# A hybrid two-layer decoder on one core: projection of token tile 0 between the norms, routing per token tile with a single gather, constant matmuls in PE's waits, and the last small-expert matmuls set behind the large ones

## Chip, cores and metric

One core of a Trainium2 chip runs the whole program. The metric is the device time of one execution in microseconds (us); where several executions are shown, their median counts. TensorE is called PE (its weight loads PEld), VectorE DVE, ScalarE ACT, GpSimd POOL, SyncE SP. SP's queue, in this kernel, does little else than start DMAs.

## What is computed

The input is x, 256 tokens of 1024 values in fp32. Each of two layers normalises x, projects it once into the inputs of four token mixers, merges their outputs through gates, projects and adds; then it normalises again and adds a feed-forward part, a dense one in layer 0 and a mixture of experts (MoE) in layer 1. Cut to that last part, where most of the time goes:

```
h = rmsnorm(x, gain)                       # 256 x 1024
logits = h @ router                        # 256 x 8
for each token: the 2 largest of 8 logits, weights = softmax of the two
y[token] = sum over its 2 experts e of weight * (silu(h @ w1[e]) * (h @ w3[e])) @ w2[e]
x = x + y                                  # w1, w3: 1024 x 3584, w2: 3584 x 1024, per expert
out = rmsnorm(x, gain)                     # after the last layer
```

All of it is fp32, and all weights come from HBM once per execution: 472 MB read.

## The kernel before

**Tiles.** The 256 tokens are two token tiles, t = 0 and 1, of 128. Weights arrive as `raw` tiles of 1 MB, one DMA each on SP's queue (`load_raw`, L125). There are 4 raw slots, 9 in the MoE part; SP starts the next load when a slot is free. A raw tile is split in two halves: ACT rounds a half to fp32r (`whi`, L164), DVE subtracts to get the remainder (`wlo`, L165). A precise product is then three matmuls, hi x hi, lo x hi, hi x lo (`mm3`, L156 to L158), or two in another arrangement (`both_parts`, L240 and L242). The activations are split in the same way: `hp`, `gTr` and `gTl`, `xer` and `xel`.

**Norms.** `norm_rows` (L193) squares on ACT, takes a square root on ACT and a reciprocal on DVE, and multiplies by x and the `gain` broadcast on DVE into `hh` (L207). `turn_half` (L217) turns hh by PE transposes into `pt`; ACT and DVE split that into `hp`. `norm_T` does both token tiles before it returns; the mixer layer begins with it. Its first product is `t_group(256, ...)`, whose matmuls write `pst`, 24 for each token tile; the next ones are `psw`. `small_loads` brings the layer's constants (sm, gln, bs, mc, cst) on POOL's queue.

**MoE.** `moe` (L667) normalises both token tiles (`hhm`), turns them (`hTm`), and multiplies by the router (`pl`, L696); the logits are turned back by a transpose (L699). DVE ranks the 8 logits (gt, eq, rank, `sel`); matmuls with a triangle and with ones give each token's position in its expert (`pp`) and the counts (`pc`). `order` sorts experts by count, so that large ones (128 slots) are paired with small ones (64 slots); `posp` are the positions in that order. `G` is the one-hot matrix of slots, and `psg` (L835) gathers the tokens: G times the split h (`htp`). Expert 0 always comes first, so its G needs no order: the kernel gathers expert 0's 128 slots first and the paired small expert's 64 in a second pass. `psgt` turns G. Loads of other experts' weights have addresses read from `ixi` on SP. `paired` then runs 28 steps, 4 pairs of 7 chunks: `psu` (large up), `psT`, `psd` (large down), `psq` (small up, plain fp32), `psTs`, `psds` (small down). `scatter_large` and `scatter_small` give the results back to tokens (`pssc`, two matmuls each, L899 and L900) and add to x (L902). `finish` normalises and stores.

**What sets the order.** Each engine runs its instructions in one list. A scheduler makes the lists when the program is built; by hand it is steered by `behind`, which keeps one instruction after another on the same engine, and by `hold_splits`, which holds back the splits of coming weights behind given instructions, but for the first few (`skip`).

Of the kernel before, what the change touches and what calls it, by code (L numbers as in the profile page):

```python
# [17 lines left out]
P = 128  # L18
# [77 lines left out]
def decoder_kernel(ctx, tc, x_in, consts_in, mconsts_in, bias_in, small_in, gln_in, gbs_in, norms_in, w_in,  # L96
# [24 lines left out]
    def load_raw(src, a, n):  # L121
# [3 lines left out]
        nc.sync.dma_start(raw, src)  # L125
        return raw

    def load_w(src, a, n):
# [3 lines left out]
        raw = load_raw(src, a, n)  # L132
# [17 lines left out]

    def w_rows(w, k0, nk, c0=0, n=D):
        return load_w(w[k0 * P:(k0 + nk) * P, c0:c0 + n].rearrange("(k p) n -> p k n", p=P), nk, n)

    def mm3(ps, lhs, rhs, start, stop):

        nc.tensor.matmul(ps, lhsT=lhs[0], rhs=rhs[0], start=start, stop=False)  # L156
        nc.tensor.matmul(ps, lhsT=lhs[0], rhs=rhs[1], start=False, stop=False)  # L157
        nc.tensor.matmul(ps, lhsT=lhs[1], rhs=rhs[0], start=False, stop=stop)  # L158
# [16 lines left out]
    nc.sync.dma_start(x[:, 0], x_in[0:P, :])  # L175
    gains = {0: gain_tile(0)}
    ident = cp.tile([P, P], F32, name="ident")
    make_identity(nc, ident)
# [4 lines left out]
    ones = cp.tile([P, P], F32, name="ones")  # L183
    nc.gpsimd.memset(ones, 1.0)
    cst = cp.tile([P, C_END], F32, name="cst")

    def sqrt_table(after, rows=slice(None)):

        junk = cp.tile([P, 1], F32, name="junk", tag="junk", bufs=2)
        nc.scalar.activation(junk[rows], after, AF.Sqrt, scale=0.0, bias=eps_l[rows])  # L190


    def norm_rows(ps, g, t, dst, done):  # L193
# [11 lines left out]
        for n in range(2):  # L205
            c = slice(n * 512, (n + 1) * 512)
            last = nc.vector.scalar_tensor_tensor(out=dst[:, c], in0=x[:, t, c], scalar=rs, in1=g[:, c],  # L207
                                                  op0=ALU.mult, op1=ALU.mult)
            done(n)
        return last  # L210

    def turn_half(hh, t, n):

        pt = psA.tile([P, 4, P], F32, name="pt", tag="mm")
        for k in range(4):
            kk = n * 4 + k
            nc.tensor.transpose(pt[:, k], hh[:, t, kk * P:(kk + 1) * P], ident)  # L217
        return pt

    def norm_T(ps, i):  # L220
# [6 lines left out]
        for t in range(TT):  # L227
# [4 lines left out]
            norm_rows(ps, g, t, hh[:, t], done)  # L232
        if ps is not None:
            hold_splits(ends, 2)
# [29 lines left out]
    def mixer_layer(l, h):  # L264
        with ExitStack() as lctx:
# [7 lines left out]
            def small_loads():  # L273
                q = nc.gpsimd
                q.dma_start(sm, small_in[l])
# [23 lines left out]
            def t_group(c0, evac):  # L299
                wt = [w_rows(win, 4 * i, 4, c0, 512) for i in range(2)]  # L300
                for t in range(TT):
# [4 lines left out]
                    evac(t, ps)  # L306
# [14 lines left out]
            t_group(256, evac_ab)  # L321
# [207 lines left out]
            units = [lambda: wq(0), lambda: wq(1), lambda: wk_(0), lambda: wk_(1), lambda: t_group(1792, evac_v)]  # L529
# [137 lines left out]
    def moe(i, norm_i, l, mT):  # L667
        with ExitStack() as lctx:
# [18 lines left out]
            for t in range(TT):  # L687
                def done(n):
                    marks["turned"] = nc.scalar.activation(hT[n][:, :, t * P:(t + 1) * P], turn_half(hh, t, n), AF.Copy)
                marks["normed"] = norm_rows(ps, g, t, hh[:, t], done)  # L690
            lgT = wk.tile([NE, T], F32, name="lgT", tag="gfs", bufs=1)
            for t in range(TT):
                tk = slice(t * P, (t + 1) * P)
                pl = psB.tile([NE, P], F32, name="pl", tag="ax")
                for k in range(KD):
                    nc.tensor.matmul(pl, lhsT=rt[:, k], rhs=hT[k // 4][:, k % 4, tk], start=k == 0, stop=k == KD - 1)  # L696
                nc.vector.tensor_copy(lgT[:, tk], pl)
                pl2 = psB.tile([P, NE], F32, name="pl2", tag="ax")
                nc.tensor.transpose(pl2, lgT[:, tk], ident[0:NE, 0:NE])  # L699
                nc.vector.tensor_copy(lg[:, t], pl2)  # L700
            halves = [slice(n * 512, (n + 1) * 512) for n in range(2)]
            with behind([marks["turned"], marks["normed"]]):
                for c in halves:
                    split(ht[0][:, 0, c], ht[1][:, 0, c], hh[:, 0, c])
            gains[norm_i + 1] = gain_tile(norm_i + 1)

            shp = [P, TT, NE, NE]
            oth = lg[:, :, None, :].to_broadcast(shp)
            own = lg[:, :, :, None].to_broadcast(shp)
            gt = wk.tile(shp, F32, name="gt", tag="rk", bufs=2)  # L710
            nc.vector.tensor_tensor(out=gt, in0=oth, in1=own, op=ALU.is_gt)
            eq = wk.tile(shp, F32, name="eq", tag="rk", bufs=2)
            nc.vector.tensor_tensor(out=eq, in0=oth, in1=own, op=ALU.is_equal)
            lt = cst[:, C_LT:C_LT + 64].rearrange("p (a b) -> p a b", a=NE)[:, None].to_broadcast(shp)
            nc.vector.tensor_tensor(out=eq, in0=eq, in1=lt, op=ALU.mult)
            nc.vector.tensor_tensor(out=gt, in0=gt, in1=eq, op=ALU.add)
            rank = small([P, TT, NE], "rank")
            nc.vector.tensor_reduce(out=rank, in_=gt, axis=AX.X, op=ALU.add)
            sel = small([P, TT, NE], "sel")
            nc.vector.tensor_scalar(out=sel, in0=rank, scalar1=1.5, scalar2=None, op0=ALU.is_lt)  # L720

            pp = psB.tile([P, TT, NE], F32, name="pp", tag="ax")
            tri = cst[:, C_TRI:C_TRI + 128]
            nc.tensor.matmul(pp[:, 0], lhsT=tri, rhs=sel[:, 0], start=True, stop=True)
            nc.tensor.matmul(pp[:, 1], lhsT=ones, rhs=sel[:, 0], start=True, stop=False)
            nc.tensor.matmul(pp[:, 1], lhsT=tri, rhs=sel[:, 1], start=False, stop=True)
            pc = psB.tile([P, NE], F32, name="pc", tag="ax")
            nc.tensor.matmul(pc, lhsT=ones, rhs=sel[:, 0], start=True, stop=False)
            nc.tensor.matmul(pc, lhsT=ones, rhs=sel[:, 1], start=False, stop=True)

            pos = small([P, TT, NE], "pos")
# [370 lines left out]
```

## Time and profile before

| what | us |
|---|---|
| median of 3 runs (1590.26 to 1591.65) | 1591.19 |
| profiled execution | 1589.84 |
| its span, first to last instruction | 1588.1 |
| layer 0's first psw starts | 31.43 |
| layer 1's first psw starts | 449.93 |
| first gather matmul psg starts | 669.31 |
| first psu starts | 683.72 |
| last matmul of the down projections starts its group | 1570.70 |

The page of the profile gives busy shares and groups; the waits list what an engine stood idle for (total, times, longest); the timeline gives single instructions with start, duration, engine, line, operation, what is written <- what is read, and in brackets the idle time before it with its releaser; a table by stretches (`A:B`) gives the busy time of each engine, the clock that was granted to PE (1.00 is full), the DMA share and GB/s. Matmul durations overlap, since they are pipelined: the distance between two starts tells the rate.

### The profile page before, as it was taken

Reading aid. Unit: us, or ns where it says so; the run is one execution under the profiler, and the core shown is the slowest. Engines: PE = TensorE matmul, PEld = TensorE weight load, DVE = VectorE, ACT = ScalarE, POOL = GpSimd, SP = SyncE. Lnnn points to the kernel's source line nnn. Section 1 sums busy time; section 2 is a strip of 40 time slices with the busy share of each in tenths; the row PEclk is TensorE's granted clock in tenths of the full one; section 3 lists DMA queues with packets and bytes.
Section 4 is the critical chain, followed back from the end, with each engine's and each line's share of the span. In section 5 each row is a group of like instructions: output and inputs, shape, how many; then the busy total and the mean of one; then the engine's idle time right before and its main releaser. Section 6 shows DMA issues by size and latency. Waiting matters only on the chain.

```text
span 1588.1 us, 20024 instructions
## 1 busy us (share of the span) xinstructions
PE 1531.3 (96%) x7508; PEld 1065.8 (67%) x7508; DVE 977.8 (62%) x1291; ACT 808.1 (51%) x1184; POOL 20.8 (1%) x47
## 2 busy tenths in 40 slices
PE   6999999999899999899999999999999999999997
PEld 5888897888788889776555555555555555555553
DVE  5896776665679777765445655454645554654444
ACT  5577746555464865554434534344434453444342
POOL 2000000000100000000000000000000000000000
PEclk9999999999999999989999999999999999999998
DMA  9565555555565645479998989999999999899993
GB/s 324 189 192 181 173 181 173 187 188 190 186 199 167 198 160 196 163 307 376 421 407 371 413 343 421 400 413 374 385 372 403 404 408 373 365 417 405 398 390 141
DMA packets 134890, 474.61 MB, mean 299 GB/s; under 512 B 7744, under 2 KB 77376, under 8 KB 91776
## 3 DMA queue, kind: packets, MB, share of 16 engines
q1 hardware_dynamic: 132512, 466.65, 76.2%
q0 software_dynamic: 1984, 6.08, 1.2%
q8 instruction: 61, 1.00, 0.3%
q10 hardware_dynamic: 288, 0.52, 0.1%
q14 instruction: 45, 0.37, 0.1%
HBM read 472.17 MB, written 1.05 MB: 298 GB/s over the span
## 4 chain that ended last, share of the span: by engine, by line
PE 89%; DVE 4%; ACT 4%; issue 2%; DMA 1%; SPq 0%; DVEq 0%; ACTq 0%
PE psw L240 16%; PE psq L923 14%; PE psw L242 8%; PE psu L157 7%; PE psu L158 7%; PE psu L156 6%; PE psds L944 5%; PE psd L157 3%; ACT whi L164 3%; PE psd L158 3%; DVE wlo L165 3%; PE psd L156 2%; PE psg L835 2%; PE psf L156 1%; PE psf L158 1%
## 5 line engine op out<-in xcount | busy, mean ns | idle before, releaser
L165 DVE TENSOR_TENSOR wlo<-raw,whi 128x1024 fp32r<-128x1024 f32 x546 | 647.7, 1221 | 252.8 <-ACT whi L164 249.6
L164 ACT ACTIVATE whi<-raw 128x1024 fp32r<-128x1024 f32 x546 | 554.0, 1053 | 130.4 <-PE psw L240 40.1
L240 PE MATMUL psw<-hp,whi 128*128 128x512 f32 x1088 | 388.6, 400 | 0.6 <-DVE hp L165 0.6
L242 PE MATMUL psw<-hp,wlo 128*128 128x256 f32 x1088 | 307.0, 282 | 0.0
L240 PEld LDWEIGHTS psw<-hp,whi 128*128 128x128 f32 x1088 | 205.1, 188 | 52.8 <-issue 3.3
L923 PE MATMUL psq<-raw,xs 128*64 128x512 f32 x896 | 218.6, 596 | 0.0
L242 PEld LDWEIGHTS psw<-hp,wlo 128*128 128x128 f32 x1088 | 206.3, 190 | 2.1 <-issue 1.1
L157 PE MATMUL psu<-wlo,xer 128*128 128x512 f32 x448 | 183.4, 409 | 9.5 <-DVE wlo L165 9.5
L156 PE MATMUL psu<-whi,xer 128*128 128x512 f32 x448 | 179.6, 401 | 1.3 <-DVE x L902 1.2
L158 PE MATMUL psu<-whi,xel 128*128 128x512 f32 x448 | 176.1, 393 | 0.0
L923 PEld LDWEIGHTS psq<-raw,xs 128*64 128x64 f32 x896 | 65.3, 137 | 129.0 <-issue 128.7
L925 ACT ACTIVATE gfs<-psq 64x512 f32<-64x512 f32 x28 | 16.5, 591 | 251.7 <-PE psq L923 251.7
L157 PEld LDWEIGHTS psu<-wlo,xer 128*128 128x128 f32 x448 | 84.6, 189 | 64.0 <-issue 30.0
L156 PEld LDWEIGHTS psu<-whi,xer 128*128 128x128 f32 x448 | 84.8, 189 | 41.9 <-ACT whi L164 17.0
L944 PE MATMUL psds<-raw,gTs 128*64 128x512 f32 x448 | 110.8, 604 | 0.0
L926 DVE TENSOR_TENSOR gfs<-gfs,psq 64x512 f32<-64x512 f32 x28 | 19.4, 692 | 137.7 <-ACT gfs L925 137.7
L158 PEld LDWEIGHTS psu<-whi,xel 128*128 128x128 f32 x448 | 84.8, 189 | 15.3
L157 PE MATMUL psd<-wlo,gTr 128*128 128x512 f32 x224 | 92.3, 412 | 2.1
L158 PE MATMUL psd<-whi,gTl 128*128 128x512 f32 x224 | 88.1, 393 | 0.0
L259 ACT ACTIVATE sum<-psw 128x256 f32<-128x256 f32 x120 | 44.8, 374 | 67.0 <-PE psw L242 67.0
L156 PE MATMUL psd<-whi,gTr 128*128 128x512 f32 x224 | 75.4, 413 | 2.7 <-ACT whi L164 2.7
L872 ACT ACTIVATE gfm<-psu 128x512 f32<-128x512 f32 x28 | 16.7, 597 | 119.9 <-PE psu L158 119.9
(260 smaller groups left out, 1570.4 us busy)
## 6 DMA issues: line engine op xcount, KB each, us to landing
raw<-in_moe_w_dram SPq DMA_DIRECT2D x336, 1024.0 KB, 8.2
raw<-in_dense_w_dram SPq DMA_DIRECT2D x33, 1024.0 KB, 5.3
raw<-in_w_gate_dram SPq DMA_DIRECT2D x32, 1024.0 KB, 5.4
raw<-in_w_in_dram SPq DMA_DIRECT2D x22, 1024.0 KB, 5.6
raw<-in_w_out_dram SPq DMA_DIRECT2D x8, 1024.0 KB, 5.0
raw<-in_w_br_c_dram SPq DMA_DIRECT2D x4, 1024.0 KB, 5.5
s<-in_bias_dram POOLq DMA_DIRECT2D x16, 192.0 KB, 4.2
gain<-in_norms_dram SPq DMA_DIRECT2D x5, 512.0 KB, 4.9
```

Of the source, the lines that this page charges most:

```text
L156: nc.tensor.matmul(ps, lhsT=lhs[0], rhs=rhs[0], start=start, stop=False)
L157: nc.tensor.matmul(ps, lhsT=lhs[0], rhs=rhs[1], start=False, stop=False)
L158: nc.tensor.matmul(ps, lhsT=lhs[1], rhs=rhs[0], start=False, stop=stop)
L164: return (nc.scalar.activation(hi, src, AF.Copy), nc.vector.tensor_tensor(out=lo, in0=src, in1=hi.bitcast(F32), op=ALU.subtract))
L165: nc.vector.tensor_tensor(out=lo, in0=src, in1=hi.bitcast(F32), op=ALU.subtract))
L240: nc.tensor.matmul(ps.rearrange("p a t -> p (a t)"), lhsT=w[0], rhs=act[:, k].rearrange("p a t -> p (a t)"), start=start, stop=False)
L242: nc.tensor.matmul(ps[:, 1], lhsT=w[1], rhs=act[:, k, 0], start=False, stop=stop)
L259: nc.scalar.activation(out[:, b], ps[b][:, 1], AF.Copy)
L835: nc.tensor.matmul(ps[:, b, cs], lhsT=ht[part][:, t, k * P:(k + 1) * P], rhs=self.G[:, t].rearrange("p s n -> p (s n)")[:, cs], start=n == ...
L923: nc.tensor.matmul(ps[rows], lhsT=xs[:, kk], rhs=w[:, k], start=kk == 0, stop=kk == KD - 1)
L926: nc.vector.tensor_tensor(out=gf[HI], in0=gf[HI], in1=ps[HI], op=ALU.mult)
L944: nc.tensor.matmul(acc["s"][rows], lhsT=gT[:, 2 * j + k], rhs=w[:, k, n * 512:(n + 1) * 512], start=c == 0 and j == 0 and k == 0, stop=c = ...
```

## The change

Six edits:

- **Start.** The gain of layer 0's first norm is no longer loaded as a 128 x 1024 broadcast. One row of 4 KB is loaded, and two matmuls with ones (`spread`) put it into PSUM, where DVE reads it. x's tile 0 comes in two halves, the first two raws in two pieces each, in the order row, x0, raw0, x1, raw1. The square-root table of ACT is loaded by an extra instruction ahead of the norm. Six one-element copies on POOL from raw1 into sm, gln, bs, mc and cst make the loads of these wait for raw1's first piece; the bias loads `s` stand ahead of them now.
- **Projection between norms.** `norm_T` takes a function that it calls after token tile 0; both mixer layers issue the 24 `pst` matmuls of tile 0 there, before tile 1's norm.
- **Routing per token tile.** gt, eq, rank, sel, off, pos, pp and pc are made for each token tile, at half the width, as soon as its logits are there.
- **One gather.** `order` and posp come first; G is made once for the large and the small expert, and psg runs once, 192 columns wide. Index loads from ixi are made at first use, not all at once. The splits of weights wait behind the gather's, where two raws had been split ahead.
- **Constant matmuls.** `keep_busy` multiplies ones by ones (`idle`, 128x128): 9 at the start, and 5, 3, 3, 8 and 12 in the routing.
- **The end.** The last small down projection (`psds`) is kept behind the last large one (`psd`).

```
+    def keep_busy(after, n):
+        ps = psB.tile([P, P], F32, name="idle", tag="ax")
+        for j in range(n):
+            with behind([after] if after else []):
+                after = nc.tensor.matmul(ps, lhsT=ones, rhs=ones, start=j == 0, stop=j == n - 1)
+        return after
+    busy = keep_busy(None, 6)
...
+            busy = nc.tensor.matmul(spread[n], lhsT=ones[0:1], rhs=row[:, n * 512:(n + 1) * 512], start=True, stop=True)
+    keep_busy(busy, 3)
...
             norm_rows(ps, g, t, hh[:, t], done)
+            if t == 0 and between:
+                between(h)
         if ps is not None:
-            hold_splits(ends, 2)
+            hold_splits(ends, 0 if between else 2)
...
+                if l == 0:
+                    for dst in (sm, gln, bs[:, 0], bs[:, 1], mc, cst):
+                        q.tensor_copy(dst[:, 0:1], early_raw[:, 1, 0:1])
...
-            t_group(256, evac_ab)
+            part = t_group(256, evac_ab)
+            evacs = []
+            h = norm_T(ps, 2 * l, lambda h: evacs.append(part(h, 0)))
+            evacs[0]()
+            part(h, 1)()
...
+            place, pm = order()
+            posp = by_place(pos, pm, "posp")
             first = Slots()
-            first.one_hot(0, pos[:, :, 0:1])
-            place, pm, ixi = order()
-            posp = by_place(pos, pm, "posp")
-            first.inputs(0, NSLOT)
-            first.one_hot(1, posp[:, :, NE // 2:NE // 2 + 1])
-            hold_splits([marks["G"]], 2)
...
-            first.inputs(NSLOT, NSLOT + NSMALL)
-            first.turned()
+            first.one_hot(None, posp[:, :, 0:NE:NE // 2])
...
+            expert(NE // 2)
+            first.inputs(0, NSLOT + NSMALL)
+            hold_splits(marks["x"], 2)
...
-                down_small(place_of[NE - 1], nch - 1, gTs)
+                with behind(ends):
+                    down_small(expert(NE - 1), nch - 1, gTs)
```

The lists of the engines show the moves. Each row has the line (those of the changed kernel are other numbers), the operation, what is written <- what is read, and the shape of the output.

SP's list at the very start, before; `in_w_in` is the mixers' input projection:

```order
L175 DMA x<-in_x_dram 128x1024
L172 DMA gain<-in_norms_dram 128x1024
L1040 DMA x<-in_x_dram 128x1024
L125 DMA raw<-in_w_in_dram 128x4x512 x2
L125 DMA raw<-in_w_in_dram 128x8x256 x2
```

and after:

```order
L190 DMA row<-in_norms_dram 1x1024
L192 DMA x<-in_x_dram 128x512 x2
L129 DMA raw<-in_w_in_dram 128x2x512 x2
L1114 DMA x<-in_x_dram 128x1024
L129 DMA raw<-in_w_in_dram 128x2x512 x2
L129 DMA raw<-in_w_in_dram 128x8x256 x2
```

The gain broadcast has gone, and the first raw stands ahead of x's second tile.

PE's list in the routing, from the transposes of the normed tokens to the first large up projection, before:

```order
L217 MATMUL pt<-ident,hhm 128x128 x8
L696 MATMUL pl<-hTm,rt 8x128 x8
L217 MATMUL pt<-ident,hhm 128x128 x8
L699 MATMUL pl_6270<-ident,lgT 128x8
L696 MATMUL pl<-hTm,rt 8x128 x8
L699 MATMUL pl_6283<-ident,lgT 128x8
L724 MATMUL pp<-sel,cst 128x8
L728 MATMUL pc<-sel,ones 128x8
L835 MATMUL psg<-G,htp 128x128 x32
L851 MATMUL psgt<-ident,G 128x128 x4
L835 MATMUL psg<-G,htp 128x64 x32
L156 MATMUL psu<-whi,xer 128x512
```

and after:

```order
L248 MATMUL pt<-ident,hhm 128x128 x8
L209 MATMUL idle<-ones 128x128 x5
L755 MATMUL pl<-hTm,rt 8x128 x8
L248 MATMUL pt<-ident,hhm 128x128 x8
L760 MATMUL pl_6310<-ident,lgT 128x8
L776 MATMUL pc<-sel,ones 128x8
L778 MATMUL pp<-sel,cst 128x8
L755 MATMUL pl<-hTm,rt 8x128 x8
L209 MATMUL idle<-ones 128x128 x12
L898 MATMUL psg<-G,htp 128x192 x32
L914 MATMUL psgt<-ident,G 128x128 x4
L163 MATMUL psu<-whi,xer 128x512
```

Left out are rows of the same kind (idle groups of 3, 3 and 8 and the rest of pp and pc). The router's matmuls of tile 1 now stand behind pc and pp of tile 0, and one gather stands where two stood.

PE's list at the end of the last step, before; the two psd are the two halves of the large expert's output:

```order
L944 MATMUL psds<-raw,gTs 64x512 x4
L157 MATMUL psd_11115<-wlo,gTr 128x512
L158 MATMUL psd_11115<-whi,gTl 128x512
L157 MATMUL psd_11116<-wlo,gTr 128x512
L158 MATMUL psd_11116<-whi,gTl 128x512
L944 MATMUL psds<-raw,gTs 64x512 x4
L899 MATMUL pssc<-yy,GT 128x512 x4
L900 MATMUL pssc<-yy,GT 128x512 x4
```

and after:

```order
L164 MATMUL psd_11153<-wlo,gTr 128x512
L165 MATMUL psd_11153<-whi,gTl 128x512
L1008 MATMUL psds<-raw,gTs 64x512 x4
L963 MATMUL pssc<-yy,GT 128x512 x4
L1008 MATMUL psds<-raw,gTs 64x512 x4
L964 MATMUL pssc<-yy,GT 128x512 x4
```

All of psd now stands ahead of psds, and the two halves of psds stand ahead of and within the scatter of the large expert.

More of the change, by code (lines that the diff above doesn't have):

```diff
@@ L173, in gain_tile @@
         return g
[L175 to L178, printed above, removed]
+    ones = cp.tile([P, P], F32, name="ones")
+    nc.gpsimd.memset(ones, 1.0)
     eps_r = cp.tile([P, 1], F32, name="eps_r")
@@ L182, in decoder_kernel @@
     nc.gpsimd.memset(eps_l, LN_EPS)
-    ones = cp.tile([P, P], F32, name="ones")
-    nc.gpsimd.memset(ones, 1.0)
+    row = actp.tile([1, D], F32, name="row", tag="gain")
+    nc.sync.dma_start(row, norms_in[0:1, :])
+    for n in range(2):
+        nc.sync.dma_start(x[:, 0, n * 512:(n + 1) * 512], x_in[0:P, n * 512:(n + 1) * 512])
+    ident = cp.tile([P, P], F32, name="ident")
+    make_identity(nc, ident)
     cst = cp.tile([P, C_END], F32, name="cst")
@@ L190, in sqrt_table @@
         nc.scalar.activation(junk[rows], after, AF.Sqrt, scale=0.0, bias=eps_l[rows])
+    sqrt_table(eps_r)
+    def keep_busy(after, n):
[5 more added lines that the diff above has]
+    busy = keep_busy(None, 6)
+    spread = [psB.tile([P, 512], F32, name="spread", tag="ax") for _ in range(2)]
+    for n in range(2):
+        with behind([busy]):
+            busy = nc.tensor.matmul(spread[n], lhsT=ones[0:1], rhs=row[:, n * 512:(n + 1) * 512], start=True, stop=True)
+    keep_busy(busy, 3)
+    gains = {0: None}
     def norm_rows(ps, g, t, dst, done):
@@ L690, in moe @@
                 marks["normed"] = norm_rows(ps, g, t, hh[:, t], done)
+                if t == 0:
+                    keep_busy(turned_last[0], 5)
+            halves = [slice(n * 512, (n + 1) * 512) for n in range(2)]
             lgT = wk.tile([NE, T], F32, name="lgT", tag="gfs", bufs=1)
+            pp = psB.tile([P, TT, NE], F32, name="pp", tag="ax")
+            pc = psB.tile([P, NE], F32, name="pc", tag="ax")
+            pos, sel = small([P, TT, NE], "pos"), small([P, TT, NE], "sel")
+            tri = cst[:, C_TRI:C_TRI + 128]
+            lt = cst[:, C_LT:C_LT + 64].rearrange("p (a b) -> p a b", a=NE)
+            shp = [P, NE, NE]
             for t in range(TT):
@@ L695, in moe @@
                 for k in range(KD):
-                    nc.tensor.matmul(pl, lhsT=rt[:, k], rhs=hT[k // 4][:, k % 4, tk], start=k == 0, stop=k == KD - 1)
+                    last = nc.tensor.matmul(pl, lhsT=rt[:, k], rhs=hT[k // 4][:, k % 4, tk], start=k == 0,
+                                            stop=k == KD - 1)
+                keep_busy(last, 3)
                 nc.vector.tensor_copy(lgT[:, tk], pl)
-                pl2 = psB.tile([P, NE], F32, name="pl2", tag="ax")
-                nc.tensor.transpose(pl2, lgT[:, tk], ident[0:NE, 0:NE])
+                pl2 = psA.tile([P, NE], F32, name="pl2", tag="mm")
@@ L700, in moe @@
+                last = nc.tensor.transpose(pl2, lgT[:, tk], ident[0:NE, 0:NE])
+                if t == 1:
+                    keep_busy(last, 8)
                 nc.vector.tensor_copy(lg[:, t], pl2)
[L701 to L731, printed above, removed]
@@ new lines, in moe @@
+                off = wk.tile([P, NE], F32, name="off", tag="off", bufs=1)
+                marks["off"] = nc.vector.tensor_scalar(out=off, in0=sel[:, t], scalar1=-1024.0, scalar2=1024.0,
+                                                       op0=ALU.mult, op1=ALU.add)
+                nc.vector.tensor_tensor(out=pos[:, t], in0=pp[:, t], in1=off, op=ALU.add)
+                if t == 0:
+                    with behind([marks["turned"], marks["normed"]]):
+                        for c in halves:
+                            split(ht[0][:, 0, c], ht[1][:, 0, c], hh[:, 0, c])
@@ L737, in moe @@
                     split(ht[0][:, 1, c], ht[1][:, 1, c], hh[:, 1, c])
-            nc.vector.tensor_tensor(out=pos, in0=pp, in1=off, op=ALU.add)
+            keep_busy(marks["pp"], 12)
+            gains[norm_i + 1] = gain_tile(norm_i + 1)
             iota = cst[:, C_IOTA:C_IOTA + 256].rearrange("p (s n) -> p s n", s=2)
```

100 lines of the change are left out of this document (72 added, 28 removed).

## The prediction

> **What bounds the kernel now.** I read the page's busy shares first, then the waits of PE, then a table by stages. PE is busy 96% of the span, so time can go only where PE waits or runs on a lower clock.
>
> ```profile
> PE 1531.3 (96%) x7508; PEld 1065.8 (67%) x7508; DVE 977.8 (62%) x1291; ACT 808.1 (51%) x1184; POOL 20.8 (1%) x47
> PE pt L217 <- DVE hh L207: 18.3, 5, 8.5
> ACT whi L164 <- DMA raw<-in_moe_w_dram: 20.4, 11, 5.2
> 0.00:8.00 8.00, 0.00 (x0) 0.00 (x0) 0.67 (x3) 4.20 (x7) 5.49 (x19) 1.00 0.68 247
> 8.00:16.00 8.00, 4.10 (x16) 3.00 (x16) 4.44 (x8) 2.69 (x8) 3.28 (x5) 1.00 1.03 373
> 24.00:220.00 196.00, 196.00 (x1211) 169.34 (x1210) 159.09 (x274) 127.39 (x229) 4.33 (x8) 1.00 0.59 190
> 432.00:440.00 8.00, 4.64 (x21) 3.92 (x22) 5.81 (x12) 3.91 (x9) 0.00 (x0) 0.79 0.19 69
> 666.00:670.00 4.00, 2.02 (x14) 1.96 (x14) 3.73 (x16) 0.00 (x0) 0.00 (x0) 0.80 0.00 0
> 670.00:684.00 14.00, 14.00 (x67) 14.00 (x67) 9.18 (x32) 4.41 (x11) 0.00 (x0) 0.50 0.53 217
> 684.00:700.00 16.00, 16.00 (x61) 12.99 (x61) 9.86 (x10) 11.20 (x12) 0.00 (x0) 0.85 0.55 210
> 740.00:1500.00 760.00, 741.92 (x3198) 425.04 (x3195) 404.26 (x403) 337.71 (x416) 0.00 (x0) 1.00 0.96 394
> ```
>
> The window rows give the stretch, its length, busy time of PE, weight loads, DVE, ACT and POOL, then granted clock, DMA share and GB/s. PE idles before 24 us, around 436 and around 666, and it works at clock .50 from 670 to 684. From 24 to 220 it is never idle and the DMAs have room (.59), so whatever PE gains at the start is kept. From 740 to 1500 PE is busy 97.6% and DMA .96: PE still leads, narrowly. The chain that can be shortened thus stands at four places, and the change touches all four.
>
> **1. The start.** It is bound by the landing of the first raws and by a slow PE.
>
> ```profile
> 15.80 2.00 ACT L164 ACTIVATE whi<-raw 128x1024 fp32r<-128x1024 f32 x2 [4.64 <-DMA raw<-in_w_in_dram]
> 16.89 1.23 DVE L165 TENSOR_TENSOR wlo<-raw,whi 128x1024 fp32r<-128x1024 f32 x1 [3.15 <-ACT whi L164]
> 16.91 0.79 PE L156 MATMUL pst<-whi,hp 128*128 128x512 f32 x1 [2.00 <-ACT whi L164]
> 19.36 0.63 PE L158 MATMUL pst<-whi,hp 128*128 128x512 f32 x1
> 19.79 0.63 PE L156 MATMUL pst<-whi,hp 128*128 128x512 f32 x1
> 31.21 0.39 PE L158 MATMUL pst<-whi,hp 128*128 128x512 f32 x1
> 31.43 0.39 PE L240 MATMUL psw<-hp,whi 128*128 128x512 f32 x1
> ```
>
> The first raw is split only at 15.80; the 48 pst start at 16.91, one each .43 us (19.36 to 19.79), later .22 (31.21 to 31.43), and the first psw comes at 31.43. The change takes the .5 MB gain broadcast off the queue (a 4 KB row and two matmuls replace it), loads the square-root table ahead of need, puts raw0 before x1, and makes the 1.5 MB of constants wait on POOL for raw1's first piece. Ahead of raw1's end then stand x0 .52, bias .79, raw0 1.05, x1 .52 and raw1 1.05, together 3.93 MB. With 2.0 MB moved by 8 us (247 GB/s) and 373 GB/s after it, raw1 is down at about 13.2. Its last split, 1.05 on ACT and 1.23 on DVE, ends at 15.5. Token tile 0's 24 pst and tile 1's transposes run meanwhile; the last hp of tile 1 is split by about 16.5. Tile 1's 24 pst take 24 x .225 = 5.4 when fast: psw at 22 to 23.4. I take 23.4, a gain of **8.0**. If those 24 all run at .43 (10.3 us), psw starts at 26.8 and 4.6 remains; if all goes early, 22.3 and 9.1. The 9 `idle` and 2 `spread` matmuls lie in the 8.5 us that PE waits for the first hh now. What queues on POOL behind the new wait is sm, gln, bs, mc and cst; the first reader, hb on DVE, stands behind eight wlo of the four raws in the new order, so some 3 us of transfers fit before it.
>
> **2. Entry of layer 1.** The same interleaving.
>
> ```profile
> 433.16 1.29 PE L217 MATMUL pt<-ident,hh 128*128 128x128 f32 x8 [2.12 <-DVE hh L207]
> 436.62 1.94 PE L217 MATMUL pt<-ident,hh 128*128 128x128 f32 x8 [2.17 <-DVE hh L207]
> 438.21 0.78 PE L156 MATMUL pst<-whi,hp 128*128 128x512 f32 x1
> 449.93 0.39 PE L240 MATMUL psw<-hp,whi 128*128 128x512 f32 x1
> ```
>
> Tile 0's pst can start when its hp is split, about 435.3, and fill the 2.17 us gap: 24 x .225 to 440.7, transposes of tile 1 to 442, its splits, then 24 more to about 448. That is **2.0** less than 449.93. The two extra whi and wlo that are now ready beforehand fall into gaps of ACT and DVE. Bounds: nothing (then the later halves' wlo, 1.23 each on DVE against 6 x .225 of PE per half, set the pace), and 3.5 (the 2.17 gap and the slow transposes and pst behind it).
>
> **3. The MoE routing.**
>
> ```profile
> 661.07 1.29 PE L217 MATMUL pt<-ident,hhm 128*128 128x128 f32 x8 [0.22 <-DVE hhm L207]
> 662.44 1.92 PE L696 MATMUL pl<-hTm,rt 128*8 128x128 f32 x16
> 665.54 0.29 DVE L711 TENSOR_TENSOR gt<-lg 128x128 f32<-128x128 f32 x1
> 667.04 0.17 DVE L720 TENSOR_SCALAR sel<-rank 128x16 f32<-128x16 f32 x1
> 667.33 1.29 DVE L165 TENSOR_TENSOR htp<-hhm,htp 128x512 fp32r<-128x512 f32 x2
> 668.54 0.17 DVE L738 TENSOR_TENSOR pos<-pp,off 128x16 f32<-128x16 f32 x1
> 669.31 7.06 PE L835 MATMUL psg<-G,htp 128*128 128x128 f32 x32 [0.71 <-DVE cmp L749]
> 676.90 7.01 PE L835 MATMUL psg<-G,htp 128*128 128x64 f32 x32
> 683.72 0.77 PE L156 MATMUL psu<-whi,xer 128*128 128x512 f32 x1
> 688.93 0.39 PE L156 MATMUL psu<-whi,xer 128*128 128x512 f32 x1
> 1304.76 2.82 PE L835 MATMUL psg<-G,htp 128*128 128x192 f32 x24
> L821 DVE TENSOR_TENSOR G<-cst,posp 128x512 fp32r<-128x512 f32 x3 | 2.1, 693 | 8.8 <-PE psg L835 8.8
> 675.15 85.11 SPq L125 DMA_DIRECT2D raw<-in_moe_w_dram  x32
> ```
>
> Removed: one of two passes of 32 psg, 7.01. Added: the single gather must wait for the order of experts and posp, which DVE worked out beside the first pass. Tile 1's pl now stands on PE behind pc and pp of tile 0, so behind tile 0's sel. Tile 1's transposes end at 662.36 now; three idle matmuls (.24 each, as a pl) stand before them, and tile 0's pl2 and its copy (.4) follow: logits at 663.1 or so. Four half-width operations of about .25, two htp of .65 among them, rank and sel: 665.7. Pc and pp, some .7, to 666.4, pl (1.92) to 668.3. From pl's end to gt took 1.18 (664.36 to 665.54): 669.5. Gt to sel took 1.67, at half width perhaps 1.4; htp 1.29 and pos: 672.4; five operations of about .25, and G, now the 128x512 form of .69, so the gather starts at **674.7**. The last 12 idle matmuls (2.9) are over by then. The 192-column psg took 2.82 for 24 at full clock, so 32 take 3.7, to 678.4. Transposes .5 and one whi of 1.05 (no raw is split ahead any more): psu at 679.9 against 683.72. Psu ran at half clock until 688.93 before, and those 12 matmuls cost 2.5 more than .225 each; new splits of 1.2 pace the first ones and cost some 1.4 of that. Gain 3.8 + 2.5 - 1.4 = **4.9**. Bounds: .7, everything at half clock (32 psg x .22 = 7.0, and no faster psu), and 9, tile 1's pl early and no pacing.
>
> The clock decides this term. By the shares .80 and .50 it fell near 668.4, after PE had done only 8-column matmuls since 664.36, and 14 us of back-to-back psg did not raise it. I take full clock, since the change sets 128-column matmuls into each of these waits. The Trainium skill, "TensorE: Matmul & The Clock Gate", section "What's actually happening", gives half clock after an idle window of about 3.4 us and full clock after about 3.4 us of sustained work. The fall agrees with that; the return does not, with 14 us at .50. By that rule even a cold gather would cost less (rival b).
>
> **4. The end.**
>
> ```profile
> 1567.70 1.94 PE L944 MATMUL psds<-raw,gTs 128*64 128x512 f32 x8
> 1570.70 1.94 PE L944 MATMUL psds<-raw,gTs 128*64 128x512 f32 x8
> 1572.57 1.19 PE L899 MATMUL pssc<-yy,GT 128*128 128x512 f32 x4
> 1573.32 0.69 DVE L165 TENSOR_TENSOR ys<-psds,ys 128x512 fp32r<-128x512 f32 x1 [1.05 <-ACT ys L164]
> 1574.03 5.36 DVE L902 SCALAR_TENSOR_TENSOR x<-pssc,combp,x 128x512 f32<-128x512 f32 x8
> ```
>
> With the small matmuls behind, psd ends 1.9 earlier, but the second half of psds (1.9) now stands between the two halves of pssc; the first pssc is complete about 1574.1, as now. DVE does ys's .69 inside the eight x additions rather than ahead of them. So the end comes **.6 later** (bounds: .5 earlier, 1 later).
>
> Inside the 28 MoE steps PE's work is the same, with psT, psq, psds and psd at other places among psu. Alternations between the fp32 matmuls of the small experts and the others, counted in the two orders, are 580 before and 584 now. PE's idle time from 740 to 1500 is 18.1 us, .75 a step; I leave it as it is, with 3 either way, a sixth of it.
>
> **Sum.** 8.0 + 2.0 + 4.9 - .6 = 14.3. The profiled execution took 1589.84 (span 1588.1 and 1.7 around it): 1575.5. The median shown, 1591.19, is 1.35 higher, so I predict **1576.9**.
>
> **Rivals.** (a) *Half clock through the gather*: the idle matmuls don't hold the clock, as the psg didn't raise it. For it: .50 from 670 to 684. Against: the 512-column pst at the start did raise it (.43 to .22 a matmul); what 128-column fp32 does, no row shows. The routing gains .7 instead of 4.9: 1581.1, chance .20. (b) *The clock falls and returns 3.4 us after the gather's start*: 15 psg at .22, 17 at .12, 1.7 dearer than 3.7: 1578.6, chance .05. The skill's rule named above would give this; the 14 us speak against it. (c) *Loads take the gain back*: the first dynamic raw is issued at 675.15 now, and after the change only behind G, three small DVE operations and one index load, about 676.5; the other six index loads stand on SP behind two raws. Then psq and psd wait for raws, and the routing's 4.9 is lost: 1581.8, chance .08. Against: 210 GB/s in 684 to 700 beside the 394 later, so the lost ground can be made up. (d) *The start keeps its slow end* (raw1 late, or 24 pst at .43): 3.4 lost, 1580.3, chance .08. (e) *Slower*: PE takes its list in order, and the new order inside the steps makes it wait for a raw or a split once a step. The DMA share of .96 and 11 waits of whi for raws (20.4 us) speak for little slack; the unchanged number of alternations and PE's 97.6% against it. From 17.5 us (14.3 and 3.2), .63 a step, it would be slower than before; if the .75 a step doubled and a little more, .8, 1576.9 + 22.4 = 1599.3, chance .04.
>
> **Range and chances.** My case has .55. All lost but the bounds' low ends (4.6, 0, .7, -1, -3) leaves 1.3 of gain; all high ends give 25. Both together are unlikely; 1569 to 1587 (gains 22 to 4) leaves out 2 in 10. A measurement of this kernel tells some .2% (3.2 us) from no change, so faster means below 1588.0: .90; two of (a), (c), (d) and weak terms together give within .2%: .06; slower .04.
>
> **What would show it.** First psw at 23 to 24 (26.8: rival d); psw of layer 1 some 2 us closer to the last psf; psg at about 675 in 3.6 us (7.0 and .50: rival a); psu some 4 us sooner after the last pso; PE's busy share from there on as before (less: c or e); additions of x ending .6 us later after the last psd. A drop of PE's 97.6% over the steps, or whi waits for raws above 20.4 us, would make the prediction wrong.

## The result, and the profile after

| | median us | range | ratio to before (95%) |
|---|---|---|---|
| before, measured beside it (4 runs) | 1591.42 | 1590.26 to 1591.78 | |
| changed kernel (4 runs) | 1581.01 | 1580.02 to 1582.43 | .9937 (.9919 to .9954) |

The change gains 10.4 us where 14.3 were predicted. The profiled execution of the changed kernel took 1581.67 (span 1579.9), 8.2 less than that of before. The sum below is made from these two profiles.

The first view is the page's busy shares of the changed kernel, followed by the two waits that were shown of before; the second fence is the table by stretches.

```profile
PE 1535.9 (97%) x7560; PEld 1064.1 (67%) x7560; DVE 977.9 (62%) x1298; ACT 804.3 (51%) x1184; POOL 21.7 (1%) x53
PE pt L248 <- DVE hh L235: 5.7, 3, 3.2
ACT whi L171 <- DMA raw<-in_moe_w_dram: 16.2, 11, 3.5
```

```profile
24.00:220.00 196.00, 196.00 (x1212) 169.48 (x1211) 161.37 (x276) 128.73 (x231) 4.32 (x8) 1.00 0.61 196
660.00:666.00 6.00, 6.00 (x39) 4.63 (x37) 2.05 (x10) 0.00 (x0) 0.00 (x0) 0.73 0.00 0
666.00:670.00 4.00, 3.76 (x33) 3.60 (x34) 3.55 (x13) 0.00 (x0) 0.00 (x0) 1.00 0.00 0
740.00:1500.00 760.00, 741.58 (x3186) 424.26 (x3186) 404.77 (x402) 334.51 (x413) 0.00 (x0) 1.00 0.96 394
```

PE's wait for hh fell from 18.3 us to 5.7, and the stretch before the gather ran at 1.00 where it had .80. The waits for MoE raws did not grow (16.2 after 20.4). Over the steps PE is as busy as before (741.58 of 760 after 741.92). That row alone looks like "steps unchanged". It is not: busy time says nothing of how much work was done in it. The next table cuts both executions at the same places in the work, by starts read from the timelines.

| stage, us | before | after | gain | predicted |
|---|---|---|---|---|
| to the first psw of layer 0 | 31.43 | 25.27 | 6.2 | 8.0 |
| last psf (layer 0's last product) to last pso (layer 1's mixers) | 225.37 | 225.34 | .0 | 2.0 |
| last pso to the 13th psu | 32.91 | 26.23 | 6.7 | 4.9 |
| 13th psu to the last pssc | 888.21 | 892.93 | -4.7 | -.6 |

With -.1 between the first psw and the last psf this makes 8.1. Two terms came out smaller than forecast and one larger, and the steps, put at 0, give 4.1 back beside the end's .6.

Each column is one profile, and the early stages vary between executions. Kernels of this study whose code is the changed one's up to there reach the first psw at 25.26 to 26.75, and those with its routing reach the 13th psu 24.6 to 27.7 after the last pso. So the gains of the start and of the routing are known to 1.5 us or so. The steps repeat better: end_undone and no_idle_start, with the same order up to the last step, took 892.4 and 893.1. The same stage in the table by stretches, first of before, then of the changed kernel, both from the 13th psu to the last pssc:

```profile
688.90:1577.20 888.30, 868.76 (x3745) 498.36 (x3743) 471.80 (x469) 395.61 (x483) 0.00 (x0) 1.00 0.93 383
```

```profile
676.10:1569.10 893.00, 872.07 (x3745) 498.04 (x3744) 477.48 (x486) 398.42 (x490) 0.00 (x0) 1.00 0.93 384
```

Both run 3745 matmuls, at full clock. The changed kernel keeps PE busy 3.3 us longer for them and leaves it idle 20.9 instead of 19.5. So most of the loss is no wait at all: the same matmuls take longer. (The busy time repeats within .2 in end_undone and no_idle_start, 871.8 and 872.2.) That was the question for the experiments.

### The profile page after: what moved, and what is told of

It reads as the page before. It is cut to its first block, busy times and chain, and to the rows that moved or that the text cites. A ratio compares the mean times of both kernels' runs of the same rounds, so it can differ in the third digit from the quotient of the medians.

```text
span 1579.9 us, 20157 instructions
## 1 busy us (share of the span) xinstructions
PE 1535.9 (97%) x7560; PEld 1064.1 (67%) x7560; DVE 977.9 (62%) x1298; ACT 804.3 (51%) x1184; POOL 21.7 (1%) x53
## 4 chain that ended last, share of the span: by engine, by line
PE 89%; DVE 4%; ACT 4%; issue 2%; DMA 1%; SPq 0%; DVEq 0%; ACTq 0%
PE psw L273 16%; PE psq L987 14%; PE psw L275 8%; PE psu L164 7%; PE psu L165 6%; PE psu L163 6%; PE psds L1008 5%; PE psd L164 3%; ACT whi L171 3%; PE psd L165 3%; DVE wlo L172 3%; PE psd L163 2%; PE psf L163 1%; PE psf L165 1%; PE psf L164 1%
## 5 line engine op out<-in xcount | busy, mean ns | idle before, releaser
L989 ACT ACTIVATE gfs<-psq 64x512 f32<-64x512 f32 x28 | 16.5, 590 | 261.5 <-PE psq L987 261.5
```

## The experiments

All carry the change but strict_before, and are measured beside the kernel before. "Alternations" are the places in PE's list of the MoE part where a plain fp32 matmul (psq, psds and the transposes psT, psTs and psgt) stands next to one on split operands. Counted without a fallback branch that never runs (the prediction's 580 and 584 included it) there are 319 before and 323 after. The traces, from the first psu to the last pssc, show 312 and 316; the differences between kernels come out the same from them, within two.

| run | median us | range | ratio to before (95%) |
|---|---|---|---|
| strict_before | 1556.16 | 1555.43 to 1557.16 | .9786 (.9769 to .9802) |
| strict_after | 1541.85 | 1541.03 to 1544.14 | .9700 (.9683 to .9716) |
| psq_whole | 1556.60 | 1552.94 to 1558.18 | .9795 (.9779 to .9811) |
| grouped_after | 1527.77 | 1526.21 to 1529.32 | .9605 (.9589 to .9621) |
| strict_hp_first | 1540.15 | 1537.99 to 1544.16 | .9693 (.9676 to .9709) |
| grouped_hp_first | 1525.49 | 1524.04 to 1527.28 | .9600 (.9584 to .9616) |
| hp_before_gelu | 1578.38 | 1577.09 to 1580.96 | .9928 (.9911 to .9946) |
| layer1_plain | 1583.80 | 1582.84 to 1584.08 | .9957 (.9942 to .9972) |
| no_idle_routing | 1585.55 | 1583.75 to 1586.61 | .9970 (.9959 to .9981) |
| no_idle_start | 1581.28 | 1580.86 to 1582.30 | .9944 (.9926 to .9962) |
| x1_first | 1586.96 | 1585.37 to 1587.93 | .9974 (.9964 to .9984) |
| end_undone | 1580.25 | 1579.89 to 1580.98 | .9936 (.9919 to .9954) |

### The steps: one order for both kernels

In both kernels each block of matmuls of a step is kept behind the one before it on PE, in the order in which the program writes them. The scheduler can then no longer strew psq among psu. Edit, of one of six blocks:

```
+            def keep(ins):
+                marks["pe"] = [ins]
...
+                with behind(marks["pe"]):
+                    for k in range(KD):
+                        last = mm3(ps, ...)
+                keep(last)
```

> The kernel before, with the matmuls of its 28 MoE steps kept in whole blocks (psu, psT, psds, psu, psq, psd, psTs) by order edges alone; 175 alternations between fp32 and other matmuls on PE instead of 319. Theory A (each alternation costs PE time, .2 to .3 us on average, and the order inside the steps took 4 us of the change's gain): 29 to 43 us less than the kernel before, 1548 to 1562. Theory B (the steps are set by the loads): PE waits for raws instead, and the time stays within 5 us of 1591.

> The changed kernel with the same whole blocks in the MoE steps, 175 alternations instead of 323. Theory A: 30 to 44 us less than the changed kernel, and, since both orders are then the same, 12 to 13 us less than the blocked kernel before (6.2 from the start, 6.7 from routing and clock). Theory B (the routing's gain is taken back by loads): at most 8.5 us less than the blocked kernel before, with more waits of whi for raws.

The same stage of strict_before and then of strict_after:

```profile
692.30:1544.10 851.80, 831.61 (x3745) 503.14 (x3743) 471.94 (x468) 395.99 (x483) 0.00 (x0) 1.00 0.97 400
```

```profile
676.20:1529.20 853.00, 831.55 (x3745) 501.16 (x3743) 477.96 (x486) 398.07 (x490) 0.00 (x0) 1.00 0.97 402
```

175 alternations stand in either list now. The 3745 matmuls take 831.6 us in both, equal to .06, where they differed by 3.3; and both are some 37 (before) and 40 us (after) shorter. Strict_after is 14.3 below strict_before by medians. That is a little over what was expected for equal steps, and the forecast sum itself, but not term by term: in its profile strict_before lost 2.0 more between psf and pso and 1.0 more before the 13th psu than the kernel before. Its granted clock was .50 from 433.4 to 443.7 and from 668.9 to 692.9, longer than in the kernel before (436.3 to 439.7 and 668.4 to 688.9), so about 3 of the 14.3 go with the clock and not with the order or the routing's work. The result of this pair is the busy time: with the order made equal, the loss in the steps is gone but for 1.2 us, of which the end is .6.

### The steps: psq alone

psq's 32 matmuls of a step are kept together, behind that step's last psu and ahead of the next psu and psd; nothing else is ordered. In the changed kernel they stood in 50 pieces for 28 steps (47 before), here in 28.

```
+                            with behind(marks["u"]):
+                                last = nc.tensor.matmul(ps[rows], lhsT=xs[:, kk], ...)
+                marks["q"] = [last]
...
+                with behind(marks["q"]):
+                    for k in range(KD):
+                        last = mm3(ps, ...)
```

> The changed kernel with only the psq of each step kept in one piece (28 pieces instead of 50); psds, psT and psTs stay where the scheduler puts them. Theory A in its sharper form (what costs most is the interruption of psq: .52 us on the way in, .52 on the way out): 22 pieces x 1.04 = 23 us less than the changed kernel, 1558. Rival (the cost lies evenly in all alternations, .24 each, or in the spread psds): 46 alternations fewer, 11 us less, 1570.

It is 24.4 below the changed kernel (1581.01 less 1556.60), as the theory of the order has it. The timeline of PE shows what a piece costs; first the changed kernel, in one step of which psq stands in four pieces:

```profile
751.37 0.39 PE L163 MATMUL psu<-whi,xer 128*128 128x512 f32 x1
751.68 1.07 PE L987 MATMUL psq<-raw,xs 128*64 128x512 f32 x2
752.69 0.50 PE L164 MATMUL psu<-wlo,xer 128*128 128x512 f32 x1
753.02 0.39 PE L165 MATMUL psu<-whi,xel 128*128 128x512 f32 x1
...
755.64 3.65 PE L987 MATMUL psq<-raw,xs 128*64 128x512 f32 x14
```

then psq_whole:

```profile
752.44 7.09 PE L992 MATMUL psq<-raw,xs 128*64 128x512 f32 x32
759.46 0.50 PE L163 MATMUL psd<-whi,gTr 128*128 128x512 f32 x1
```

In the whole row a psq comes every .22 (7.02 from its start to the next psd, for 32). Two in a piece of their own take 1.01 to the next psu instead of .44, and the psu on either side come at .31 and .33 instead of .23: about .75 for a piece, and no engine is named as waited for. The group rows of PE's psq add that up, of before, of the changed kernel and of psq_whole (times of all 896, counted where they don't overlap, and mean ns of one):

```profile
L923 PE MATMUL psq<-raw,xs 128*64 128x512 f32 x896 | 218.6, 596 | 0.0
```

```profile
L987 PE MATMUL psq<-raw,xs 128*64 128x512 f32 x896 | 221.0, 597 | 0.0
```

```profile
L992 PE MATMUL psq<-raw,xs 128*64 128x512 f32 x896 | 198.4, 595 | 0.0
```

One psq lasts 596 ns in each; only their overlap differs. 22 pieces fewer free 22.6 us, 1.03 each. From before to after the row grows by 2.4, the three pieces more. That is the greater part of the 3.3; of the rest, psd's 672 matmuls account for .8 (178.3 to 179.1 in all). What makes a piece dear is not shown: psq and psds differ from psu and psd both in type (plain fp32, unsplit) and in the width of their weights (64 columns, not 128), and no run parts the two.

### The steps: fewer changes still

As strict_after, but the blocks of a step in another order, so that all fp32 ones stand together (75 alternations): both parts of psu, psTs, psT, psq, psds, psd.

> The blocked changed kernel with the blocks of a step in the order psu, psu, psTs, psT, psq, psds, psd, so that fp32 and other matmuls alternate 75 times instead of 175. Theory A alone (an alternation costs PE .24 us, and nothing else binds): 24 us less than strict_after, 1518. Theory C (after the first 148 alternations the loads have become the bound: 99% DMA share, 410 GB/s, 839 us from the first psu to the last psq for 352 MB): within 5 us of strict_after, with more or longer waits of whi for raws.

It is 14.1 below strict_after, with 100 alternations fewer. The stage of grouped_after and the steady stretch inside it, then its wait for raws, then the steady stretch of the changed kernel:

```profile
676.00:1515.90 839.90, 821.40 (x3745) 507.42 (x3743) 475.91 (x485) 402.97 (x490) 0.00 (x0) 1.00 0.99 408
700.00:1480.00 780.00, 764.23 (x3496) 473.68 (x3494) 438.09 (x436) 369.02 (x448) 0.00 (x0) 1.00 1.00 416
```

```profile
ACT whi L171 <- DMA raw<-in_moe_w_dram: 3.1, 7, 0.7
```

```profile
700.00:1480.00 780.00, 762.17 (x3285) 436.98 (x3284) 416.32 (x413) 345.29 (x427) 0.00 (x0) 1.00 0.95 393
```

PE's busy time falls by 10.2 (831.55 to 821.40) and its idle time from 21.5 to 18.5. So an alternation here is worth .1, against .26 from before to strict_before (37.2 for 144) and .58 in psq_whole (26.7 for 46): alternations are not one price, and those that cut psq up are the dear ones. Both expectations missed: a saving of .24 for each, 24 in all, was too much for what was left, and the loads did not hold the gain within 5. The DMAs now move 416 GB/s at a share of 1.00. Yet PE is idle no longer than it was, so the loads are not shown to hold this version; by the share they have little room left for a faster one. The waits of whi for raws say little by themselves: they were 97.6 us in strict_after and 3.1 here, with PE idle 21.5 and 18.5.

In all, 872.1, 845.4, 831.6 and 821.4 us of PE for the same 3745 matmuls (changed kernel, psq_whole, strict, grouped), with 18.5 to 21.5 idle in each: the steps of this kernel are bound by PE, and PE by its own order.

### The entry of layer 1

The forecast let the splits of hp for tile 1 follow its transposes at once. ACT's timeline of the changed kernel, and PE's:

```profile
435.49 1.28 ACT L362 ACT_TABLE_LOAD   x1 [6.01 <-PE pst L165]
436.78 0.38 ACT L362 ACTIVATE vg<-pst 128x256 f32<-128x256 f32 x1
437.06 1.08 ACT L171 ACTIVATE hp<-pt 128x512 fp32r<-128x512 f32 x2
```

```profile
435.24 1.03 PE L248 MATMUL pt<-ident,hh 128*128 128x128 f32 x8
437.70 0.50 PE L163 MATMUL pst<-whi,hp 128*128 128x512 f32 x1 [1.43 <-ACT hp L171]
```

Tile 0's pst end just before tile 1's transposes; ACT takes their Gelu (vg) first, with its table load, and PE stands 1.43 us for hp. In hp_before_gelu the reading of tile 0's product out of PSUM (vg on ACT, zb on DVE) is kept behind tile 1's hp:

```
-            evacs[0]()
+            with behind(ring["after"]):
+                evacs[0]()
```

> The changed kernel, with the Gelu and copy of token tile 0's first product (vg, zb) kept behind token tile 1's hp on ACT and DVE, in layer 1. Theory: the entry of layer 1 gained nothing because ACT loads the Gelu table and does vg (1.3 + .4 us) before tile 1's hp, so that PE waits 1.4 us: the wait goes, first psw after layer 1's entry comes 1.4 to 1.8 us sooner, total 1579. Rival: tile 1's transposes, which stand behind tile 0's 24 pst, set it alone: less than .5 us.

```profile
434.63 1.09 ACT L171 ACTIVATE hp<-pt 128x512 fp32r<-128x512 f32 x2 [5.88 <-PE pt L248]
435.73 1.28 ACT L362 ACT_TABLE_LOAD   x1
```

From the last psf to the last pso it takes 222.54 instead of 225.34. About 1.0 of these 2.8 is the clock. The stretch at the entry, of the changed kernel and then of end_undone, whose code is the same there:

```profile
428.00:432.00 4.00, 4.00 (x14) 3.30 (x14) 2.77 (x5) 1.13 (x3) 0.00 (x0) 0.61 0.10 32
```

```profile
428.00:432.00 4.00, 3.97 (x17) 2.95 (x17) 2.69 (x5) 0.67 (x2) 0.00 (x0) 1.00 0.20 59
```

End_undone, psq_whole and grouped_after entered at full clock, and took 224.39, 224.35 and 224.31. What is left for the order on ACT is 1.8. By medians hp_before_gelu gains 2.6; the ranges of the two overlap by 1 us.

Layer1_plain leaves the projection of tile 0 between the norms out of layer 1 only:

```
-            h = norm_T(ps, 2 * l, lambda h: evacs.append(part(h, 0)))
-            evacs[0]()
+            if l == 0:
+                h = norm_T(ps, 2 * l, lambda h: evacs.append(part(h, 0)))
+                evacs[0]()
+            else:
+                h = norm_T(ps, 2 * l)
+                part(h, 0)()
```

> The changed kernel with layer 1 entered as before (both token tiles normed, then the 48 pst), judged by the time from the last psf to the last pst, since the order of the MoE steps comes out another way (331 alternations instead of 323). Theory: the entry as changed gains nothing while ACT's Gelu table load stands ahead of tile 1's hp: 19.0 us from the last psf to the second psw, as in the kernel before, and within .5 of the changed one (19.6 less the two psw pulled forward). By the alternations the total is 2 us above the changed kernel. Rival: the interleaving is worth the predicted 2 us: 2 us longer from psf to psw.

It took 225.32 there, as the changed kernel did, and entered at the lower clock as that did: without hp first, the interleaving brings nothing in layer 1 that is seen. By medians the run is 2.8 above the changed kernel; in its profile the difference lies elsewhere, 1.4 between the last pso and the first psu (24.83 after 23.41) and .7 in the steps, where its list has 331 alternations. The 1.4 go with the clock. With the same code in the routing, tile 1's pl took 3.58 at half clock in hp_before_gelu (24.65 to the first psu) and as long in layer1_plain, and 1.91 in strict_hp_first (21.79). First hp_before_gelu, then strict_hp_first:

```profile
656.98 3.58 PE L756 MATMUL pl<-hTm,rt 128*8 128x128 f32 x16
```

```profile
656.80 1.91 PE L756 MATMUL pl<-hTm,rt 128*8 128x128 f32 x16
```

The granted clock was .50 for 6.8 us there in the first two (654.9 to 661.8 and 657.5 to 664.3), for 3.4 in the changed kernel (659.8 to 663.2), and 1.00 throughout in strict_hp_first.

With hp first, the two best orders were run again:

> The blocked changed kernel (strict_after) with tile 1's hp kept ahead of the Gelu in layer 1. Theory: both gains add: 1.8 us from the last psf to the psw, MoE steps as in strict_after: 1539.5 to 1540.5. Rival: the loads in the MoE steps, now the bound, take it back: within .5 of strict_after.

> The grouped kernel with tile 1's hp ahead of the Gelu in layer 1, the two best versions together. Theory: 1.8 us less than the grouped one, 1526. Rival (the loads, at 416 GB/s from 700 to 1480 now the bound, take it back): within .5 of 1527.8.

They gain 1.7 and 2.3 on strict_after and grouped_after by medians, with ranges that overlap; both reach the last pso 222.6 after the last psf (225.3 and 224.3 without hp first). Grouped_hp_first is the best version of the study, 4.0% below the kernel before and 3.5% below the changed one (1525.49 against 1581.01).

### The routing

no_idle_routing leaves out the constant matmuls there (5, 3, 3, 8 and 12).

> The changed kernel without the 31 constant matmuls of the routing. Clock theory: the granted clock falls to half before the gather as in the kernel before; 32 psg take 7.0 instead of 3.6, the first 12 psu 5.2 instead of 2.8: 5 to 6 us more, 1586 to 1587. Rival (the single gather alone brings the gain, the idle matmuls only fill): within 1 us of the changed kernel.

PE's timeline around the gather, of the changed kernel and then of no_idle_routing, and the table by stretches of the latter:

```profile
658.68 0.39 PE L776 MATMUL pc<-sel,ones 128*128 128x8 f32 x2 [2.63 <-DVE sel L775]
659.44 3.29 PE L755 MATMUL pl<-hTm,rt 128*8 128x128 f32 x16
663.92 2.05 PE L209 MATMUL idle<-ones 128*128 128x128 f32 x16
669.34 3.79 PE L898 MATMUL psg<-G,htp 128*128 128x192 f32 x32 [0.24 <-DVE ix L820]
673.33 0.48 PE L163 MATMUL psu<-whi,xer 128*128 128x512 f32 x1
```

```profile
666.18 5.96 PE L892 MATMUL psg<-G,htp 128*128 128x192 f32 x32 [3.10 <-DVE ix L814]
672.01 0.47 PE L163 MATMUL psu<-whi,xer 128*128 128x512 f32 x1
```

```profile
664.00:668.00 4.00, 1.82 (x9) 1.85 (x9) 2.39 (x9) 0.00 (x0) 0.00 (x0) 0.50 0.00 0
668.00:672.00 4.00, 4.00 (x26) 4.00 (x26) 1.15 (x3) 1.71 (x5) 0.00 (x0) 0.66 0.74 274
672.00:680.00 8.00, 8.00 (x40) 6.59 (x39) 7.53 (x17) 7.79 (x11) 0.00 (x0) 1.00 0.64 246
```

The clock of the changed kernel falls as well, near 660, after PE had waited 2.63 us for sel, and tile 1's pl takes 3.29 instead of 1.92. But it is back at 1.00 before the gather, which takes 3.8. Without the constant matmuls the gather starts at half clock and takes 5.96. Of the 2.2 lost there 1.2 are won ahead of it, where fewer matmuls stand: the 13th psu comes 27.14 after the last pso, against 26.23. So in this pair the constant matmuls are worth .9 in the routing, not the 5 to 6 that the clock theory gave them; and 27.14 lies within the 24.6 to 27.7 that kernels with them took, so even the .9 is not shown. The median's +4.5 is not theirs: in the profile the steps took 3.4 longer (896.30 after 892.93), for 3746 matmuls, one more by the cut:

```profile
675.10:1571.40 896.30, 874.62 (x3746) 499.26 (x3745) 477.32 (x483) 399.38 (x490) 0.00 (x0) 1.00 0.93 382
```

With instructions left out of the routing, the scheduler ordered the steps behind it otherwise: PE is busy 2.6 longer at the same count of alternations, 323. By the time from one start to the next, psu take 1.3 of that more and psds .9, psq nothing.

### The start

x1_first sets the load of token tile 1 ahead of raw0's, on the thought that tile 1's late norm delays psw.

```
-    early.append(load_raw(row_blocks(w_in[0], 0, 4, 256, 512), 4, 512, 2))
     nc.sync.dma_start(x[:, 1], ...)
+    early.append(load_raw(row_blocks(w_in[0], 0, 4, 256, 512), 4, 512, 2))
```

> The changed kernel with the load of x's second token tile put ahead of the first raw. Theory: what is late at the start is token tile 1 (its squares at 12.1, hh at 15.8, transposes at 17.3, behind the splits of raw0 and raw1 on ACT and DVE): first psw 1 to 2 us sooner than 25.3, though the first pst start later. Rival (the landing of raw1 sets it): first psw not sooner than 25.3. The order of the MoE steps comes out another way here, so the start is judged by the first psw alone.

The first psw came at 27.37, 2.1 later than in the changed kernel and .6 later than in any kernel with the changed start as it is, not earlier: the first pst waits for raw0's split until 11.78 (it starts at 9.40 in the changed kernel). The rest of this run's loss is in the steps again (897.5 from the 13th psu to the last pssc). In the changed kernel itself:

```profile
10.63 1.06 ACT L171 ACTIVATE whi<-raw 128x1024 fp32r<-128x1024 f32 x1 [1.27 <-DMA raw<-in_w_in_dram]
12.07 0.62 ACT L228 ACTIVATE hh<-x 128x512 f32<-128x512 f32 x1
...
17.27 1.04 PE L248 MATMUL pt<-ident,hh 128*128 128x128 f32 x8
18.56 0.50 PE L163 MATMUL pst<-whi,hp 128*128 128x512 f32 x1 [0.25 <-ACT hp L171]
25.27 0.62 PE L273 MATMUL psw<-hp,whi 128*128 128x512 f32 x2
```

ACT waits for raw0's second half, splits it, and only then squares x1 (12.07); tile 1's transposes follow at 17.27, and 29 pst, not 24, stand between them and psw (18.56 to 25.27, .23 each). no_idle_start leaves out the 9 constant matmuls at the start.

> The changed kernel without the 9 constant matmuls at the start; PE's order in the MoE steps is the same. Theory: the start is set by when token tile 1's hp is there (18.6 us in the changed kernel) and by the 29 pst behind it, not by the clock: first psw still at 25.3 to 26, total within .7 us. Rival (the idle matmuls warm the clock and that sets the start): first psw at 27 to 28.

Its first psw came at 24.64, sooner than in any other run, and its total is that of the changed kernel (1581.28 against 1581.01), so those 9 bring nothing that is seen.

### The end

> The changed kernel without the edit at the end (the last psds may again stand among the last psd); PE's order in the MoE steps up to there is the same. Theory: the edit costs .6, so the time from the last psTs to the last pssc is .6 shorter here and the total within 1 us of the changed kernel, on the faster side. Rival: the edit gains (psd and yy ready 1.9 sooner): this kernel 1 us slower.

Its edit takes away the line `with behind(ends):` around the last down_small. With an unchanged order up to there, it reaches the last pssc .58 sooner after the 13th psu (892.35 after 892.93), all of it behind the last psTs (12.77 to the last pssc, against 13.33, and 13.37 in no_idle_start). By medians it is .8 faster, inside the ranges of the two. DVE's last additions, of end_undone and of the changed kernel:

```profile
1564.11 5.36 DVE L966 SCALAR_TENSOR_TENSOR x<-pssc,combp,x 128x512 f32<-128x512 f32 x8
```

```profile
1565.35 1.41 DVE L966 SCALAR_TENSOR_TENSOR x<-pssc,combp,x 128x512 f32<-128x512 f32 x2 [3.83 <-PE pssc L964]
1566.68 0.69 DVE L172 TENSOR_TENSOR ys<-psds,ys 128x512 fp32r<-128x512 f32 x1
1567.28 4.04 DVE L966 SCALAR_TENSOR_TENSOR x<-pssc,combp,x 128x512 f32<-128x512 f32 x6
```

The split of ys stands inside the eight additions, as forecast.

## Why the prediction was right or wrong

**The time** fell into the range (1569 to 1587), the sign was right, and the likeliest value was 4.1 us low. The total lies on that of rivals (a) (half clock through the gather, 1581.1) and (c) (loads take the gain back, 1581.8), and near (d) (the start at its slow end, 1580.3). By place, (a) and (c) did not happen: the gather ran at full clock, and whi waited less for raws than before. That the total fell into the range is thus in part luck: terms off by 1.8, 2.0 and 4.1 one way and 1.8 the other. The agreement of a total proves no mechanism. One slip in the working: rival (a) and the low bound of the routing count .7 for the routing at half clock, where its own terms, 3.8 less 7.0 - 3.7, give .5.

**The steps** are where it failed. The step was "alternations 580 before and 584 now", hence 0 with 3 either way, and with it 0 gain or loss for another order. The count rose by 4, as said, and the inference was wrong: the price depends on which kinds meet and on how many pieces psq is cut into (47 and 50), which went uncounted. Measured, the term is -4.1 beside the end: 3.3 of busy PE and .8 idle. The signs named beforehand, PE's busy share and whi's waits for raws, showed nothing of it. Strict order removes the 3.3, which shows the order as the cause; psq's pieces account for 2.4 of it. Rival (e) named the right place, PE's order within a step, but as a wait for raws or splits, at over 17.5 us. What exactly makes x1_first and no_idle_routing 3.8 and 2.6 busier than the changed kernel, at 325 and 323 alternations and 50 pieces of psq like it, stays open; it lies in psu and psds (1.7 and 1.9 in x1_first, from start to start), and not in psq.

**The start** was mis-sized: 6.2 for 8.0, inside the bounds 4.6 to 9.1. Tile 1's hp was put at 16.5 and came at 18.5; by the lists, because splits of raw0 and raw1 stand among tile 1's norm on ACT and DVE. That is argued: the one run that moved x1 forward moved the first pst back as well. And 29 pst are left then, not 24.

**The entry of layer 1** was mis-sized, 0 in the profile (at half clock for 3.4 us, as the kernel before was) and 1.0 in those at full clock, for 2.0, because the forecast missed that ACT would load the Gelu table and do vg ahead of hp. With hp first it is 2.8, of which some 1.0 is the clock.

**The routing** was right in kind and better in size: psu 4.3 sooner after the last pso (3.8 forecast), and the first 12 psu 2.4 faster (1.1 forecast), at full clock and hardly paced by splits. The reason "128-column matmuls hold the clock" was only half right: the clock fell in a place that has none. Without them it came back as well (1.00 from 660.5 to 663.9 in no_idle_routing) and fell a second time (.50 from 663.9 to 670.7), which no kernel with them shows in its routing. Part of the term is fortune: the same code took from 1.6 less to 1.5 more in other executions.

**The end** came .6 later, as forecast (end_undone).

## What to carry to other kernels

Where an engine is busy almost all the time, compare the busy time of the same number of its instructions between two cuts in the work, not its share: here 3745 matmuls took 820 to 876 us by their order alone. Where a kernel mixes plain fp32 matmuls with others, try keeping them in long runs on PE: here a scheduler that filled gaps with them cost 40 us of busy PE and saved .5 of idle time. And any edit upstream can reshuffle such an order, so a difference of a few us is to be placed by stage before it is credited to the edit.

## What the runs showed of the hardware that was not expected

- A run of fp32 psq cut off from its like costs .75 (one piece in the timeline) to 1.0 us (22.6 us for 22 pieces), though each matmul lasts the same 596 ns.
- The clock came back within 5 us in no_idle_routing (.50 in 664 to 668, .66 in 668 to 672, 1.00 in 672 to 680, with 192-column psg from 666.18), while 14 us of 128- and 64-column psg did not raise it before the change. The Trainium skill, "TensorE: Matmul & The Clock Gate", section "What's actually happening", gives about 3.4 us of sustained work for the return; the first case is compatible with that, the second is not.
- At the start the clock came to stay at no fixed time: by the pst rate (.43 to .23 us a matmul) at 13.04 in no_idle_start, 14.44 in the changed kernel and 18.33 in x1_first. In the changed kernel it seems to have been up once before: the spread matmuls, which start at 3.94 behind 6 constant ones in both, took 2.20 us there and 3.78 in x1_first; from 7.8 to 14.7 the granted clock was .50 again.
- Half clock at the entry of layer 1 and in the routing comes and goes between executions of the same code (0, 3.4 or 6.8 us of it), and with it 1 to 3 us of the time.
- The loads of one core reached 416 GB/s at a DMA share of 1.00.
